# Input stage of a two-network kernel: modulation matmuls of five blocks in rows of eight, and part of the mLSTM keys multiplied in the first two blocks

## The chip, the cores and the metric

The kernel runs on one core of a Trainium2 chip. The metric is the device time of one execution in microseconds (us), as the median of several runs.

## The reference, cut to what matters

Two networks' blocks run one after the other on 256 tokens of width D = 2048. The part that the change touches is the input of the first one: a modulation vector for the tokens and one for the context, a normalised and modulated hidden state for each, and one projection `w_in` whose columns are cut into the inputs of two recurrent mixers (GLA and mLSTM).

```python
mod = (c_act @ w_mod + b_mod)[:, None, :]
mod_c = (cc_act @ w_mod + b_mod)[None, None, :]
sh1, sc1, gt1, sh2, sc2, gt2 = jnp.split(mod, 6, axis=-1)
csh1, csc1, ... = jnp.split(mod_c, 6, axis=-1)
h  = rmsnorm(x, g_norm1) * (1 + sc1) + sh1
hc = rmsnorm(ctx, g_norm1) * (1 + csc1) + csh1
z = jnp.einsum('btd,dp->btp', h, w_in)        # for h and for hc
gq, gk, gv, gg, glr, mq, mk, mv, mo, mgate = jnp.split(z, PROJ_SPLITS, axis=-1)
```

`gk` (GLA keys, 512 columns), `gv` (GLA values, 1024), the gates, and `mk` (mLSTM keys, columns 3600 to 4111 of `w_in`) are needed for tokens and context.

## The kernel before, in words

All inputs are float32. A weight is loaded as 512 KB of raw float32 (`load_raw`, L172; four buffers), cut by ScalarE into a high part `wh` (L187) and by VectorE into the rest `wl` (L188), and a product is made of three matmuls (`mm3`, L208 to L210). VectorE is DVE in the profile, ScalarE ACT, TensorE PE, SyncE SP.

The input stage walks over the 2048 rows of the weights in eight blocks of two k-tiles of 128 rows. For each block, `mod_pe` (L465) computes the modulation of the block's 256 columns for shift and scale, for both vectors at once: four tiles `wm` of 1 MB each hold four k-tiles of `w_mod`; for each of them PE runs a row of four 32-column matmuls into four column strips (L481). After the fourth come a copy by ACT (L486), four transposes (L488), a sum over the strips by DVE (L490) and the bias and gain (L497, L499). `hidden` transposes the tokens (L305) and modulates them (L312, L314), then splits them (L290, L291). `pieces` multiplies the block's weights: GLA keys into four PSUM accumulators that stay open over all blocks; GLA values, two halves, evacuated per block by a copy (block one, L612) or an add (L614) into tiles in SBUF; then the gates (L630). The modulation of block b + 1 is a generator that is stepped between the pieces of block b, at every second piece.

`weights(b, i)` loads the units of a block. Every call of `units` also ticks two background streams: `mods`, which computes the other modulation sections with DVE (L514, L516) from 512 KB loads of `w_mod` and ends each with a bias row on PE (L523), and `side`, recurrent work that fills gaps. What `mods` has not done by the end of the mixing stage is done at once (L1197, `while self.mods_done < 12: self.mods.step()`).

After the eight blocks, `k_evac` (L674) takes GLA's keys out of PSUM by ACT (L678), transposes two of the four (L684), and then the keys stage multiplies the mLSTM keys: `a_form` over all 16 k-tiles, eight units, again with `k_evac`; the queries follow.

The big tiles share one set of 14 buffers of 8 KB per partition (`b8`): the token tiles, the hidden states, the GLA values, the modulation tiles `wm`, later tiles of the recurrences. A tile's first load or write waits for the last reader of the tile that had the buffer before. SP issues the loads in the order in which the program is written; the order of the other engines comes from a scheduler that runs when the program is built. Each engine, SP too, works strictly in its order, so a load that waits for a buffer holds every load behind it.

Of the kernel before, what the change touches and what calls it, by code (L numbers as in the profile page):

```python
# [106 lines left out]
class Kern:  # L107
# [357 lines left out]
    def mod_pe(self, c0, n, secs):  # L465
# [4 lines left out]
        pt = self.psm()[:, :m]  # L470
        for k0 in range(0, 16, 4):
            wm = self.b8((P, 4, m))
            for i, sec in enumerate(secs):
                src = a["w_mod"][0, k0 * P:(k0 + 4) * P, sec * D + c0:sec * D + c0 + n]
                nc.sync.dma_start(wm[:, :, i * n:(i + 1) * n], src.rearrange("(k p) n -> p k n", p=P))

            ins = None
            for j in range(4):
                k = k0 + j
                with self.tc.issue_after(ins) if ins is not None else contextlib.nullcontext():  # L480
                    ins = nc.tensor.matmul(pt[32 * j:32 * j + 32, :], self.cs[:, 2 * k:2 * k + 32], wm[:, j, :],  # L481
                                           start=k < 4, stop=k >= 12, tile_position=(0, 32 * j)).ins
            if k0 < 12:
                yield 1
# [76 lines left out]
    def mix_in(self):  # L561
# [27 lines left out]
        gk_acc = [self.acc() for _ in range(4)]  # L589
        gvc = self.b8((P, 2, 1024))  # L590
# [5 lines left out]
        def mod_block(b):  # L596
            lo, hi = blocks[b]
            return self.mod_pe(lo * P, (hi - lo) * P, (0, 1))
# [7 lines left out]
        def pieces(b):  # L606
# [12 lines left out]
            for half in range(2):  # L619
                for tt in order:  # L620
                    acc = self.ps()
                    self.a_form([acc], [forms[tt]], ws[b, 1 + half], kts[0], kts[-1])
                    add((gvc if tt < 2 else self.gv)[:, tt % 2, half * 512:(half + 1) * 512], acc)
                    yield 1

# [10 lines left out]
        def weights(b, i):  # L636
            if b < nb:
                ws[b, i] = list(self.units(w, 512 + 512 * i, 512, range(*blocks[b])))
# [9 lines left out]
        weights(0, 2)  # L648
        for b in range(nb):
# [7 lines left out]
            for i, _ in enumerate(pieces(b)):  # L657
                if i == 4:
                    weights(b + 1, 1)
                if i == 8:  # L660
                    weights(b + 1, 2)
                if i % 2 == 0:
# [11 lines left out]
        def k_evac(accs, dst, scale):  # L674
            kc = []
            for tt in range(4):
                t = self.t2()
                nc.scalar.activation(out=t, in_=accs[tt], func=AF.Copy, scale=scale)  # L678
# [19 lines left out]
        self.a_form(accs, forms, self.units(w, 3600, 512, range(16)), 0, 15)  # L698
        self.mkc = k_evac(accs, self.mk, float(P) ** -0.5)
# [1155 lines left out]
```

## Time and profile before

| | |
|---|---|
| median of 3 runs | 2664.92 us (2662.52 to 2669.27) |
| profiled execution | 2672.57 us, span 2670.4 us |
| mean granted clock of PE | 0.991 |
| PE busy | 2603.5 us, 97% |
| DVE busy | 1846.4 us, 69% |
| ACT busy | 1281.8 us, 48% |
| queue of SP, share of 16 DMA engines | 63.9%, 548.54 MB |

Busy shares are averages over stages that differ. The input stage is the first 215 us or so of the span. A timeline row gives the start, the length and in brackets the idle time of the engine just before, with what ended it; matmuls overlap their neighbours, so the distance of two starts tells more than a length. "PEclk" is the granted clock as a share of 2.4 GHz; 0.50 is the lower level, 1.2 GHz.

### The profile page before, as it was taken

Reading aid. Unit: us, or ns where it says so; the run is one execution under the profiler, and the core shown is the slowest. Engines: PE = TensorE matmul, PEld = TensorE weight load, DVE = VectorE, ACT = ScalarE, POOL = GpSimd, SP = SyncE. Lnnn points to the kernel's source line nnn. Section 1 sums busy time; section 2 is a strip of 40 time slices with the busy share of each in tenths; the row PEclk is TensorE's granted clock in tenths of the full one; section 3 lists DMA queues with packets and bytes.
Section 4 is the critical chain, followed back from the end, with each engine's and each line's share of the span. In section 5 each row is a group of like instructions: output and inputs, shape, how many; then the busy total and the mean of one; then the engine's idle time right before and its main releaser. Section 6 shows DMA issues by size and latency. Waiting matters only on the chain.

```text
span 2670.4 us, 37499 instructions
## 1 busy us (share of the span) xinstructions
PE 2603.5 (97%) x14093; PEld 2190.4 (82%) x14093; DVE 1846.4 (69%) x3006; ACT 1281.8 (48%) x2008; POOL 26.5 (1%) x52
## 2 busy tenths in 40 slices
PE   5999999999899999999999999999999999999999
PEld 3666888877778888888888988888888889998888
DVE  4466678787778988857856867677755566666665
ACT  2223323344365555544534554555544455657553
POOL 1000000000000000000000000000000000000000
PEclk8999999999999999999999999999999999999999
DMA  9775466678876666666675666556665567645664
GB/s 333 246 239 173 143 211 199 226 224 265 274 260 220 210 220 206 226 218 205 204 243 179 215 190 189 190 189 189 197 232 189 185 208 215 166 143 173 201 217 159
DMA packets 345271, 558.89 MB, mean 209 GB/s; under 512 B 30692, under 2 KB 129178, under 8 KB 342402
## 3 DMA queue, kind: packets, MB, share of 16 engines
q1 hardware_dynamic: 339800, 548.54, 63.9%
q10 hardware_dynamic: 4746, 7.11, 0.7%
q8 instruction: 110, 1.80, 0.3%
q0 software_dynamic: 544, 0.86, 0.1%
q14 instruction: 71, 0.58, 0.1%
HBM read 541.75 MB, written 14.69 MB: 208 GB/s over the span
## 4 chain that ended last, share of the span: by engine, by line
PE 82%; DMA 8%; DVE 6%; ACT 2%; issue 2%; SPq 1%; POOL 0%; ACTq 0%; DVEq 0%
PE acc L237 20%; PE acc L210 10%; PE acc L208 10%; PE acc L209 10%; PE acc L238 10%; PE mod L237 5%; DMA raw<-in_w_in_dram 3%; PE mod L238 2%; PE mod L209 2%; PE mod L210 2%; PE mod L208 2%; DMA raw<-in_w_mod_dram 2%; DVE wl L188 2%; DMA raw<-in_w_out_dram 1%; DVE ev L516 1%
## 5 line engine op out<-in xcount | busy, mean ns | idle before, releaser
L188 DVE TENSOR_TENSOR wl<-raw,wh 128x1024 fp32r<-128x1024 f32 (+4 forms) x804 | 965.7, 1205 | 578.2 <-ACT wh L187 575.5
L187 ACT CAST wh<-raw 128x1024 fp32r<-128x1024 f32 (+4 forms) x804 | 829.6, 1036 | 1068.0 <-PE acc L210 345.7
L237 PE MATMUL acc<-b,wh 128*128 128x512 f32 x2336 | 821.1, 394 | 0.0
L238 PE MATMUL acc<-b,wl 128*128 128x256 f32 x2336 | 634.4, 281 | 1.1 <-DVE wl L188 1.0
L208 PE MATMUL acc<-wh,b 128*128 128x512 f32 (+3 forms) x1580 | 585.3, 373 | 10.0 <-ACT b L290 7.6
L209 PE MATMUL acc<-wl,b 128*128 128x512 f32 (+3 forms) x1580 | 586.6, 371 | 7.5 <-DVE wl L188 7.3
L210 PE MATMUL acc<-wh,b 128*128 128x512 f32 (+3 forms) x1580 | 576.2, 370 | 1.1 <-DVE b L291 0.6
L237 PEld LDWEIGHTS acc<-b,wh 128*128 128x128 f32 x2336 | 434.1, 188 | 88.9 <-issue 0.7
L238 PEld LDWEIGHTS acc<-b,wl 128*128 128x128 f32 x2336 | 438.9, 188 | 15.0 <-DVE wl L188 2.4
L208 PEld LDWEIGHTS acc<-wh,b 128*128 128x128 f32 x1580 | 298.8, 189 | 71.8 <-ACT b L290 9.4
L209 PEld LDWEIGHTS acc<-wl,b 128*128 128x128 f32 x1580 | 299.2, 189 | 62.1 <-DVE wl L188 12.6
L210 PEld LDWEIGHTS acc<-wh,b 128*128 128x128 f32 x1580 | 297.0, 189 | 55.6 <-DVE b L319 4.0
L516 DVE SCALAR_TENSOR_TENSOR ev<-raw,cs,ev 128x512 f32<-128x512 f32 x240 | 179.4, 747 | 59.1 <-DMA raw<-in_w_mod_dram 56.4
L237 PE MATMUL mod<-b,wh 128*128 128x512 f32 x576 | 215.5, 396 | 0.6 <-DVE t L249 0.6
L238 PE MATMUL mod<-b,wl 128*128 128x256 f32 x576 | 161.5, 280 | 0.7 <-DVE wl L188 0.7
L237 PEld LDWEIGHTS mod<-b,wh 128*128 128x128 f32 x576 | 108.4, 188 | 23.5 <-DVE t L249 1.1
L1367 DVE SCALAR_TENSOR_TENSOR t<-t,convw,t 128x189 f32<-128x189 f32 (+2 forms) x344 | 126.9, 423 | 0.0
L238 PEld LDWEIGHTS mod<-b,wl 128*128 128x128 f32 x576 | 108.3, 188 | 3.9 <-DVE wl L188 1.1
L208 PE MATMUL mod<-wh,b 128*128 128x512 f32 (+2 forms) x274 | 96.9, 354 | 0.0
L209 PE MATMUL mod<-wl,b 128*128 128x512 f32 (+2 forms) x274 | 96.7, 353 | 0.0
L210 PE MATMUL mod<-wh,b 128*128 128x512 f32 (+2 forms) x274 | 96.5, 352 | 0.0
L290 ACT CAST b<-t 128x256 fp32r<-128x256 f32 x123 | 47.2, 405 | 64.2 <-DVE t L314 44.1
(357 smaller groups left out, 2469.0 us busy)
## 6 DMA issues: line engine op xcount, KB each, us to landing
raw<-in_w_up_dram SPq DMA_DIRECT2D x160, 512.0 KB, 4.5
raw<-in_w_mod_dram SPq DMA_DIRECT2D x128, 512.0 KB, 4.5
raw<-in_pool_w_in_dram SPq DMA_DIRECT2D x128, 512.0 KB, 3.8
raw<-in_w_in_dram SPq DMA_DIRECT2D x96, 512.0 KB, 4.9
raw<-in_w_down_dram SPq DMA_DIRECT2D x83, 512.0 KB, 4.8
b<-in_w_mod_dram SPq DMA_DIRECT2D x64, 512.0 KB, 7.9
raw<-in_pool_w_out_dram SPq DMA_DIRECT2D x64, 512.0 KB, 4.0
raw<-in_ple_w_gate_dram SPq DMA_DIRECT2D x64, 512.0 KB, 3.9
```

What stands on the lines that cost most here:

```text
L187: nc.scalar.copy(wh[:, :n], raw[:, :n])
L188: nc.vector.tensor_tensor(out=wl[:, :n], in0=raw[:, :n], in1=wh[:, :n].bitcast(F32), op=ALU.subtract)
L208: mm(out, lh, rh, start=first, stop=False)
L209: mm(out, lh, rl, start=False, stop=False)
L210: mm(out, ll, rh, start=False, stop=last)
L237: mm(acc, wh[:, i, o], f.both(kt), start=kt == k_first, stop=False)
L238: mm(acc[:, :T], wl[:, i, o], f(kt)[0], start=False, stop=kt == k_last)
L290: nc.scalar.copy(h, src)
L516: nc.vector.scalar_tensor_tensor(out=ev, in0=rv[:, i, :], scalar=cc, in1=ev, op0=ALU.mult, op1=ALU.add)
L1367: nc.vector.scalar_tensor_tensor(out=ov[:, r0:r1, c0:c1], in0=uv[:, r0 + dy:r1 + dy, c0 + dx:c1 + dx], scalar=tap(ky, kx), in1=ov[:, r0:r1 ...
```

## The change

The modulation function gets a flag that is set for blocks three to seven. With it, two `wm` tiles are loaded before one row of eight matmuls, the newer tile's four first. The first two blocks load a fourth unit of weights (columns 3600 to 4111 of `w_in`) and multiply it, 24 matmuls a block; the result goes into a new tile `mk0` in the set of 14 buffers, by copies in block one and adds in block two. The keys stage then starts at k-tile 4 (six units in place of eight), and its evacuation adds `mk0` on DVE before ACT's scaling.

```diff
--- before.py
+++ after.py
@@ -462,24 +462,32 @@
             self.rows_T([cw[r0:r1, :]] + last, self.convw, r0)
         self.convb = self.convw[:, 9 * NFC:]
 
-    def mod_pe(self, c0, n, secs):
+    def mod_pe(self, c0, n, secs, pairs):
 
 
         nc, a = self.nc, self.a
         m = n * len(secs)
         pt = self.psm()[:, :m]
+        wms = []
         for k0 in range(0, 16, 4):
             wm = self.b8((P, 4, m))
             for i, sec in enumerate(secs):
                 src = a["w_mod"][0, k0 * P:(k0 + 4) * P, sec * D + c0:sec * D + c0 + n]
                 nc.sync.dma_start(wm[:, :, i * n:(i + 1) * n], src.rearrange("(k p) n -> p k n", p=P))
+            wms.append(wm)
+            if pairs and len(wms) == 1:
+                yield 1
+                continue
 
             ins = None
-            for j in range(4):
-                k = k0 + j
-                with self.tc.issue_after(ins) if ins is not None else contextlib.nullcontext():
-                    ins = nc.tensor.matmul(pt[32 * j:32 * j + 32, :], self.cs[:, 2 * k:2 * k + 32], wm[:, j, :],
-                                           start=k < 4, stop=k >= 12, tile_position=(0, 32 * j)).ins
+            for wm, k1 in ((wms[-1], k0), (wms[0], k0 - 4))[:len(wms)]:
+                for j in range(4):
+                    k = k1 + j
+                    with self.tc.issue_after(ins) if ins is not None else contextlib.nullcontext():
+                        ins = nc.tensor.matmul(pt[32 * j:32 * j + 32, :], self.cs[:, 2 * k:2 * k + 32], wm[:, j, :],
+                                               start=k0 < 8 and k1 == k0 if pairs else k0 == 0,
+                                               stop=k0 == 12 and (k1 < k0 or not pairs), tile_position=(0, 32 * j)).ins
+            wms = []
             if k0 < 12:
                 yield 1
         ev = self.t2()[:, :m]
@@ -587,6 +595,9 @@
 
         gates = self.t2((112, 2, T))
         gk_acc = [self.acc() for _ in range(4)]
+
+        early = 2
+        mk0 = self.b8((P, 4, 512))
         gvc = self.b8((P, 2, 1024))
         self.gv = self.b8((P, 2, 1024))
 
@@ -595,7 +606,7 @@
 
         def mod_block(b):
             lo, hi = blocks[b]
-            return self.mod_pe(lo * P, (hi - lo) * P, (0, 1))
+            return self.mod_pe(lo * P, (hi - lo) * P, (0, 1), 1 < b < nb - 1)
 
         def hidden(b, ti):
             kts = list(range(*blocks[b]))
@@ -622,6 +633,12 @@
                     self.a_form([acc], [forms[tt]], ws[b, 1 + half], kts[0], kts[-1])
                     add((gvc if tt < 2 else self.gv)[:, tt % 2, half * 512:(half + 1) * 512], acc)
                     yield 1
+            if b < early:
+                for tt in order:
+                    acc = self.ps()
+                    self.a_form([acc], [forms[tt]], ws[b, 3], kts[0], kts[-1])
+                    add(mk0[:, tt, :], acc)
+                    yield 1
 
             acc = self.ps().rearrange("p (i t) -> p i t", i=2)[:112]
             for i, hx in enumerate((hc, hl)):
@@ -635,7 +652,7 @@
         ws = {}
         def weights(b, i):
             if b < nb:
-                ws[b, i] = list(self.units(w, 512 + 512 * i, 512, range(*blocks[b])))
+                ws[b, i] = list(self.units(w, 512 + 512 * i if i < 3 else 3600, 512, range(*blocks[b])))
         for _ in mod_block(0):
             pass
         hidden(0, 0)
@@ -646,6 +663,7 @@
         weights(0, 1)
         wg = self.gate_weights(w)
         weights(0, 2)
+        weights(0, 3)
         for b in range(nb):
             mods = mod_block(b + 1) if b + 1 < nb else iter(())
 
@@ -659,6 +677,8 @@
                     weights(b + 1, 1)
                 if i == 8:
                     weights(b + 1, 2)
+                    if b + 1 < early:
+                        weights(b + 1, 3)
                 if i % 2 == 0:
                     next(mods, None)
                 if i == 8 and b + 1 < nb:
@@ -671,11 +691,15 @@
         self.gkq = self.b8((P, 2, 4, T))
         self.queries = False
 
-        def k_evac(accs, dst, scale):
+        def k_evac(accs, dst, scale, part=None):
             kc = []
             for tt in range(4):
                 t = self.t2()
-                nc.scalar.activation(out=t, in_=accs[tt], func=AF.Copy, scale=scale)
+                if part is None:
+                    nc.scalar.activation(out=t, in_=accs[tt], func=AF.Copy, scale=scale)
+                else:
+                    nc.vector.tensor_tensor(out=t, in0=accs[tt], in1=part[:, tt, :], op=ALU.add)
+                    nc.scalar.mul(t, t, scale)
                 if tt < 2:
                     kc.append(t)
                     continue
@@ -695,8 +719,8 @@
         self.side.set(self.gla_context(gkc, gvc), SIDE["keys"])
         self.mk = self.t4((P, 4, T))
         accs = [self.acc() for _ in range(4)]
-        self.a_form(accs, forms, self.units(w, 3600, 512, range(16)), 0, 15)
-        self.mkc = k_evac(accs, self.mk, float(P) ** -0.5)
+        self.a_form(accs, forms, self.units(w, 3600, 512, range(2 * early, 16)), 2 * early, 15)
+        self.mkc = k_evac(accs, self.mk, float(P) ** -0.5, mk0)
 
 
         self.side.set(self.gla_scores(), SIDE["queries"])
```

In the order of PE, at the turn from block one to block two, before. L481 are the modulation rows, L630 the gates, L488 the transposes of the modulation, `acc` the GLA keys (of block two here), `ps` other products:

```order
L210 MATMUL ps_424<-wh_256,b_11_120 128x512
L481 MATMUL mod_272<-b_71_342,cs 32x512 x4
L630 MATMUL ps_432<-b_11_120,t_53_246 112x256 x4
L630 MATMUL ps_432<-b_15_124,t_53_246 112x256 x4
L488 MATMUL mod_272<-cst,t_72_349 128x128 x4
L481 MATMUL mod_454<-b_93_455,cs 32x512 x4
L208 MATMUL acc_131<-wh_262,b_15_124 128x512
L209 MATMUL acc_131<-wl_263,b_15_124 128x512
L208 MATMUL acc_132<-wh_262,b_15_124 128x512
L209 MATMUL acc_132<-wl_263,b_15_124 128x512
L208 MATMUL ps_487<-wh_315,b_15_124 128x512
```

And with the change, where L487 is the row, L496 the transposes, the products `ps_445`, `ps_453` and `ps_461` are of the mLSTM keys:

```order
L210 MATMUL ps_437<-wh_257,b_11_120 128x512
L487 MATMUL mod_279<-b_75_349,cs 32x512 x4
L208 MATMUL ps_445<-wh_263,b_15_124 128x512
L209 MATMUL ps_445<-wl_264,b_15_124 128x512
L210 MATMUL ps_445<-wh_263,b_15_124 128x512
L208 MATMUL ps_445<-wh_263,b_15_124 128x512
L209 MATMUL ps_445<-wl_264,b_15_124 128x512
L210 MATMUL ps_445<-wh_263,b_15_124 128x512
L496 MATMUL mod_279<-cst,t_76_356 128x128 x4
L208 MATMUL ps_453<-wh_263,b_15_124 128x512
L209 MATMUL ps_453<-wl_264,b_15_124 128x512
L210 MATMUL ps_453<-wh_263,b_15_124 128x512
```

Six rows further on, where the first GLA keys of block two come:

```order
L208 MATMUL ps_461<-wh_263,b_11_120 128x512
L209 MATMUL ps_461<-wl_264,b_11_120 128x512
L210 MATMUL ps_461<-wh_263,b_11_120 128x512
L208 MATMUL acc_131<-wh_269,b_15_124 128x512
L209 MATMUL acc_131<-wl_270,b_15_124 128x512
```

Six products of block one's mLSTM keys now stand between the last row and the transposes. Behind the transposes come 18 more, the first 12 of them ahead of the first GLA keys of block two (`acc`), and the gates only after them.

In the order of PE, the first two modulation rows of block eight, before, and the bias row of the mods stream:

```order
L210 MATMUL ps_1463<-wh_1283,b_18_127 128x512
L481 MATMUL mod_1430<-b_267_1431,cs 32x512 x4
L481 MATMUL mod_1430<-b_268_1450,cs 32x512 x4
L523 MATMUL ps_1475<-ev_1025,cst 1x512
L208 MATMUL ps_1495<-wh_1283,b_18_127 128x512
```

And with the change:

```order
L210 MATMUL ps_1540<-wh_1360,b_18_127 128x512
L487 MATMUL mod_1507<-b_282_1508,cs 32x512 x4
L487 MATMUL mod_1507<-b_283_1527,cs 32x512 x4
L531 MATMUL ps_1552<-ev_1102,cst 1x512
L208 MATMUL ps_1572<-wh_1360,b_18_127 128x512
```

The rows still stand together, and the bias row behind them.

In the order of SP, the loads of block eight's modulation tiles (b8, two loads each) and those around them, before, with the numbers of tiles:

```order
L475 DMA b8_267_1431<-in_w_mod_dram 128x4x256 x2
L475 DMA b8_268_1450<-in_w_mod_dram 128x4x256 x2
L172 DMA raw_270_1471<-in_w_mod_dram 128x2x512
L525 DMA t2_272_1477<-in_b_mod_dram 1x512
L172 DMA raw_274_1482<-in_w_in_dram 128x2x512
L475 DMA b8_277_1488<-in_w_mod_dram 128x4x256 x2
L475 DMA b8_280_1511<-in_w_mod_dram 128x4x256 x2
L172 DMA raw_286_1546<-in_w_mod_dram 128x2x512
L172 DMA raw_287_1550<-in_w_in_dram 128x2x512
```

And with the change:

```order
L476 DMA b8_282_1508<-in_w_mod_dram 128x4x256 x2
L476 DMA b8_283_1527<-in_w_mod_dram 128x4x256 x2
L172 DMA raw_285_1548<-in_w_mod_dram 128x2x512
L533 DMA t2_287_1554<-in_b_mod_dram 1x512
L172 DMA raw_289_1559<-in_w_in_dram 128x2x512
L476 DMA b8_292_1565<-in_w_mod_dram 128x4x256 x2
L476 DMA b8_295_1588<-in_w_mod_dram 128x4x256 x2
L172 DMA raw_301_1623<-in_w_mod_dram 128x2x512
L172 DMA raw_302_1627<-in_w_in_dram 128x2x512
```

The order is the same, but the buffers are not. Before, the first and third of the four tiles have one buffer and the second and fourth another, so that the third waits for the first's row. With the change all four have the same one, and each waits for the row of the tile before it.

## Rows read from the trace of the kernel before

**Rows 1.** The page's first part: busy time and share of each engine.
```profile
PE 2603.5 (97%) x14093; PEld 2190.4 (82%) x14093; DVE 1846.4 (69%) x3006; ACT 1281.8 (48%) x2008; POOL 26.5 (1%) x52
```

**Rows 2.** Windows: time, PE, PEld, DVE, ACT, POOL busy, then PEclk, DMA share, GB/s.
```profile
64.00:68.00 4.00, 1.65 (x4) 1.36 (x5) 3.27 (x8) 2.11 (x6) 0.00 (x0) 0.71 1.08 392
68.00:72.00 4.00, 4.00 (x10) 3.11 (x10) 0.61 (x2) 0.12 (x1) 0.00 (x0) 0.50 1.05 362
72.00:76.00 4.00, 4.00 (x18) 3.15 (x16) 0.00 (x0) 0.00 (x0) 0.00 (x0) 0.94 0.10 30
```

**Rows 3.** PE's timeline: start, us, engine, line, operation, out<-in, count, [idle before].
```profile
62.85 1.06 PE L481 MATMUL mod<-b,cs 128*32 128x512 f32 x8 [0.44 <-DVE sm L490]
66.35 0.80 PE L208 MATMUL acc<-wh,b 128*128 128x512 f32 x1 [2.44 <-ACT b L290]
66.94 0.63 PE L209 MATMUL acc<-wl,b 128*128 128x512 f32 x1
67.37 0.63 PE L208 MATMUL acc<-wh,b 128*128 128x512 f32 x1
67.80 0.63 PE L209 MATMUL acc<-wl,b 128*128 128x512 f32 x1
...
72.06 0.59 PE L209 MATMUL acc<-wl,b 128*128 128x512 f32 x1
...
74.13 0.39 PE L208 MATMUL acc<-wh,b 128*128 128x512 f32 x1
74.36 0.40 PE L209 MATMUL acc<-wl,b 128*128 128x512 f32 x1
```

**Rows 4.** PE's timeline about a modulation row of four (eight records).
```profile
76.00 0.39 PE L210 MATMUL acc<-wh,b 128*128 128x512 f32 x1
76.31 1.07 PE L481 MATMUL mod<-b,cs 128*32 128x512 f32 x8
77.31 0.50 PE L208 MATMUL acc<-wh,b 128*128 128x512 f32 x1
77.65 0.39 PE L209 MATMUL acc<-wl,b 128*128 128x512 f32 x1
```

**Rows 5.** PE's timeline about a modulation row of eight.
```profile
51.58 1.92 PE L481 MATMUL mod<-b,cs 128*32 128x512 f32 x16
53.44 0.66 PE L305 MATMUL ps<-cst,b 128*128 128x128 f32 x4
```

**Rows 6.** PE's timeline, block eight's modulation to its first matmul.
```profile
194.70 1.92 PE L481 MATMUL mod<-b,cs 128*32 128x512 f32 x16
196.99 1.02 PE L523 MATMUL ps<-ev,cst 128*1 128x512 f32 x2 [0.37 <-DVE ev L516]
...
201.29 1.06 PE L481 MATMUL mod<-b,cs 128*32 128x512 f32 x8 [0.30 <-DMA b<-in_w_mod_dram]
...
205.72 1.06 PE L481 MATMUL mod<-b,cs 128*32 128x512 f32 x8
...
215.16 0.50 PE L208 MATMUL acc<-wh,b 128*128 128x512 f32 x1 [0.34 <-ACT b L290]
```

**Rows 7.** SP's timeline over the same modulation's loads: issues.
```profile
174.40 4.89 SPq L475 DMA_DIRECT2D b<-in_w_mod_dram  x4
...
195.82 2.02 SPq L475 DMA_DIRECT2D b<-in_w_mod_dram  x4
```

**Rows 8.** DVE's timeline at the end of block seven.
```profile
205.62 0.49 DVE L514 TENSOR_SCALAR ev<-raw,cs 128x512 f32<-128x512 f32 x1 [0.93 <-DMA raw<-in_w_mod_dram]
206.02 0.68 DVE L614 TENSOR_TENSOR b<-ps,b 128x512 f32<-128x512 f32 x1
...
214.13 0.54 DVE L314 TENSOR_SCALAR t<-ps,mod,mod 128x256 f32<-128x256 f32 x1
```

**Rows 9.** The chain at the end of the mixing stage: start, length, what.
```profile
730.69 10.66 DMA raw<-in_w_mod_dram
```

**Rows 10.** PE's timeline at the end of the mixing stage.
```profile
725.81 1.84 PE L543 MATMUL ps<-cst,ev 128*128 128x2 f32 x8 [4.41 <-DVE ev L516]
```

## The prediction

> **What bounds the kernel now.** I read the page's first part, then the core's windows through the input stage, then TensorE's (PE's) timeline at each edit, then the queue of SP, then VectorE (DVE). PE is busy 97% of the span [rows 1], so work taken off another engine is worth nothing and an idle microsecond of PE is a lost one, unless a later wait gives it back. The input stage has two parts. Until 72 us the loads are the limit: the DMA engines are full in every window shown up to there, and PE waits and then runs at half clock, 0.50 granted from 68 to 72 us [rows 2]. From 72 us DMA is nearly idle in the window shown and PE sets the time. "Within 0.3%" is 8 us here, about what can be told from no change.
>
> The profiled execution took 2672.57 us, 7.65 more than the median of the runs, 2664.92. The sum below is made against 2672.57 and 7.65 is then taken off.
>
> **The early key products, at the front.** The change moves 48 matmuls of 512 columns from the keys stage into blocks one and two, 24 each. Their number is unchanged, so at full clock they cost PE nothing. They pay where they stand in a hole. The hole is the turn from block one to block two: PE waits 0.44 us for DVE before one modulation row and 2.44 us for ScalarE's (ACT's) cast of the new hidden tokens, then starts matmuls 0.43 us apart instead of 0.23 [rows 3]. Fourteen matmuls start at the slow spacing between 66.35 and 72.06, which costs 14 x 0.20 = 2.8 us. The order rows of PE after the change put 12 of the new matmuls between the transposes of block two's modulation and the first matmul that needs the new hidden tokens, and move a modulation row away from there. Before, the transposes ended and the tokens were ready some 2.9 us of waiting and one row of 1.0 us later, 3.9 us; 12 x 0.23 = 2.8 us covers all but 1.1, and with so short a wait PE should not fall to half clock. Gain: 0.44 + 2.44 - 1.1 + 2.8 = **-4.6 us**. What the step adds: two loads of 512 KB, ahead of others on a full DMA. At the 392 GB/s of [rows 2] each takes 1.3 us, and if all of it shows, 2.7 us of the gain are gone. I count it at nothing, because the longer PE work of these blocks gives the later tiles the same time; without that cover the term is -2. The eight copies and adds of 0.68 us on DVE [rows 8] lie beside PE work. Range -6 (the wait covered whole) to -1 (late, and half the slow stretch back).
>
> **The rows of eight.** A row of four stands between two triples: from the last matmul before it to the second one after it are 77.65 - 76.00 = 1.65 us, of which two normal spacings are 0.46, so a row costs 1.19 us [rows 4]. A row of eight, found in the old program where two rows happened to meet, takes 1.86 us to the next matmul, against 1.00 for the row of four [rows 4, 5]; so eight cost 1.19 + 0.86 = 2.05, and each pair saves 2 x 1.19 - 2.05 = 0.33 us. There are ten pairs (two in each of five blocks) and one is cut apart by gate matmuls in the new order: **-3.1 us**, range -4 to 0. A pair needs two tiles at once, so a tile's load may be later than before; between the first pair's row and the second are some 30 matmuls, 7 us, against 5.4 us for a load (next part). That covers it.
>
> **The last block's modulation.** This is the cost that the diff does not show. The new tile mk0 lives in the same set of 14 buffers as the modulation tiles, from block one until the keys are done. The order rows of SP and the order of buffers say what this does for block eight, which is not paired: its four tiles A, B, C, D had two buffers, and now have one. B's load can only be issued after A's row has read the buffer, while PE's order has B's row right behind A's. Before, A and B had landed long ago, and SP issued C and D together when the rows of A and B were through [rows 6, 7].
>
> I reckon from T0, the end of A's row. How long a load of 1 MB takes when its issue is awaited: C was issued at 195.82 and its row began at 201.29 after a wait for it [rows 6, 7], 5.4 us with D queued behind. The other bound is 1.05 MB at 392 GB/s [rows 2], 2.7 us, with no latency at all; I take 5.4, since it is the same transfer.
> By the Trainium skill (DMA: Bandwidth & Descriptors, Anatomy of one DMA) a transfer, on the path through GpSimd, takes a fixed 2.0 us plus its bytes at 436 GB/s. That makes an estimate of 4.4 us for such a tile, and the sum below would be 1 us lower; the trace's 5.4 us has other loads beside it.
> - B lands at T0 + 5.4. PE idles that long and then runs at half clock. Row B ends at T0 + 6.5, and only then is C issued, to land at T0 + 11.9. PE meanwhile has one bias row of 1.0 us and 12 matmuls at 0.43, 5.1 us: row C at about T0 + 12.6, over at T0 + 13.6.
> - D is issued then and lands at T0 + 19.0; 24 matmuls cover that.
> - Behind D on SP stand the weights of block eight and the mods stream's loads. Before, from D's issue (the third of four issues that start at 195.82, about 196.8) to the first matmul of block eight at 215.16 were 18.3 us, through D's row, a raw load that DVE waited for until 205.62, and DVE's normalising at 214.13 [rows 6 to 8]. The same from T0 + 13.6 gives T0 + 31.9.
> Before, T0 was about 195.7 and block eight's first matmul 19.5 us later. So +12.4. After the second idle PE is at half clock again for about as long as at the front, of which I charge 1.1 of 2.8 us, because PE has another wait there anyhow. **+13.5 us.** Bounds: only B's wait less the old waits that go away, +3; C idle as well and the whole half clock, +19. Counting from D's row instead of its issue gives +10.
>
> **Keys to queries.** The keys' evacuation gains four adds of DVE, 0.68 us each [rows 8], ahead of ACT's scaling. Gla's state matmuls wait for the last of them, since the state tile takes mk0's buffer. The queries' matmuls cover most; I take **+1.5**, from 0 to +5.
>
> **The mods stream.** Its loads step with the weight units, and the keys stage has two units fewer. The two steps are made up in the burst that ends the mixing stage, where PE waits 4.41 us for DVE at 725.81 and one load stands 10.66 us on the chain [rows 9, 10]. Two loads at 1.3 us on the path: **+2.5**, from 0 (the burst hidden) to +6 (half such a turn more).
>
> **Sum:** -4.6 - 3.1 + 13.5 + 1.5 + 2.5 = +9.8; 2672.57 + 9.8 - 7.65 = 2674.7, say **2675 us**.
>
> **The rivals.**
> 1. *Not slower: the last block absorbs its single buffer.* If DVE's chain does not wait behind D, the stall is B's wait of 5.4 less the waits of 0.37 and 0.30 that it replaces and others like them, +3, and the two tails are hidden: -4.6 - 3.1 + 3 = -4.7, **2660 us**. It decides for "not slower" as soon as the last block loses under 8 us with the tails at nothing. For: VectorE has idle time in that stretch. Against: [rows 8] show that it did wait for the raw load behind D. With the front at -6, the pairs at -4 and the last block at +2 it goes to 2657, the edge of faster by over 0.3%.
> 2. *In between.* The stall counted from D's row, +10, and one tail hidden: -4.6 - 3.1 + 10 and 1.5 or 2.5, +4 to +5, **2669 to 2670 us**.
> 3. *The tails bite.* The forecast's stall, with the keys turn at +5 and the burst at +6: **2682 us**; with the last block at +19 up to 2687.
> 4. *The pairs stall.* If second pairs' tiles land later than the 30 matmuls, each of ten pairs costs its load less 7 us and a fall to half clock instead of saving 0.33; two such stalls of 3 us add 6: **2681 us**.
>
> **Chances.** Forecast 0.34 (2671 to 2679), rival 1 0.26, rival 2 0.18, rivals 3 and 4 together 0.22. Slower by over 0.3% begins at 2673: nearly all of rivals 3 and 4 and 0.8 of the forecast, 0.48. Faster by over 0.3% ends at 2657, the better half of rival 1 with several terms at their good ends: 0.14. Within: 0.38. The range from 2657 to 2687 leaves out the best of rival 1 and the worst of 3 and 4. The likeliest case alone has 2671 to 2679.
>
> **What would show it.** In the new profile: a wait of about 1 us in place of 2.44, and no window at 0.50 clock, at the first block's turn; rows of eight in blocks three to seven with nothing idle before them; in the last block B's row 5 us or more behind A's, released by a load, a half clock window behind it, and about 32 us from A's row to block eight's first matmul. If A's and B's rows still stand together, or the distance stays near 20 us, the main term is wrong and rival 1 holds. If a row of eight waits for a load, it is rival 4.

## The result, and the profile after

| | before | with the change |
|---|---|---|
| median | 2665.64 us (2662.52 to 2669.27, 4 runs) | 2705.99 us (2704.56 to 2708.22, 4 runs) |
| ratio | | 1.0152, 95% interval 1.0134 to 1.0169 |
| profiled execution | 2672.57 us, span 2670.4 | 2706.64 us, span 2704.6 |

The change costs 40 us where 10 were forecast, and lies outside the range. The stall in the last block came as forecast. What was missed lies 400 us later, in a stage whose code the change does not touch.

The page's first part of the changed kernel, against [rows 1]: PE's share has not moved, which is why such a share cannot be read as "nothing waits".

```profile
PE 2615.3 (97%) x14093; PEld 2198.5 (81%) x14093; DVE 1855.4 (69%) x3018; ACT 1282.1 (47%) x2007; POOL 26.2 (1%) x52
```

Where the 34 us of the two profiled executions lie can be told by four landmarks that stand in both programs: the first row of block eight's modulation (called A), the last row of the mLSTM's sums (L1120, L1144 in the new numbering; the end of the recurrences), the first row scale of the second network (L1335, now L1359), and the end. The early matmuls moved 48 x 0.23 = 11.0 us across A, and are taken off or added on. Each kernel has one trace, and executions of the kernel before alone lie between 2662.5 and 2677.8 us, so a difference of a few us in one stretch tells little.

| stretch | before | after | difference, moved work taken off |
|---|---|---|---|
| start to A | 194.7 | 205.3 | -0.5 |
| A to the last L1120 | 379.0 | 380.8 | +12.9 |
| last L1120 to first L1335 (mixing stage, feed-forward) | 930.2 | 944.8 | +14.6 |
| first L1335 to the end of the span | 1166.6 | 1173.7 | +7.1 |

The last line is the second network, which nothing here reaches; it comes up again at the end.

**The turn from block one to block two.** The windows that answer to [rows 2], in the changed kernel:

```profile
64.00:68.00 4.00, 2.87 (x13) 1.96 (x12) 3.85 (x10) 0.66 (x2) 0.00 (x0) 1.00 1.08 379
68.00:72.00 4.00, 4.00 (x19) 3.24 (x18) 2.59 (x6) 2.62 (x6) 0.00 (x0) 1.00 1.09 377
72.00:76.00 4.00, 4.00 (x28) 2.92 (x30) 1.92 (x2) 0.00 (x0) 0.00 (x0) 1.00 0.54 156
```

PE's timeline there, which answers to [rows 3]:

```profile
64.46 0.50 PE L208 MATMUL ps<-wh,b 128*128 128x512 f32 x1 [0.35 <-DVE b L623]
...
66.91 0.50 PE L208 MATMUL ps<-wh,b 128*128 128x512 f32 x1 [0.78 <-DVE b L623]
...
68.41 0.39 PE L208 MATMUL acc<-wh,b 128*128 128x512 f32 x1
```

The wait of 2.44 us is gone, two of 0.35 and 0.78 us (1.13 together; 1.1 was forecast) stand in its place, and the window at 0.50 is at full clock.

Most of the gain is gone again at A. In block five PE waits twice for DVE at the transposes of a later stage's weights (L382) and runs at 0.50 of the clock behind that, from 158 to 161 us; the kernel before has no such wait there:

```profile
156.53 0.26 PE L382 MATMUL ps<-cst,t 46*128 46x46 f32 x1 [0.53 <-DVE convw L383]
...
157.86 0.80 PE L208 MATMUL ps<-wh,b 128*128 128x512 f32 x1 [1.08 <-DVE convw L383]
```

**The last block.** PE's timeline with the four rows and block eight's first matmul, against [rows 6]:

```profile
205.27 1.07 PE L487 MATMUL mod<-b,cs 128*32 128x512 f32 x8
211.98 1.93 PE L487 MATMUL mod<-b,cs 128*32 128x512 f32 x8 [5.65 <-DMA b<-in_w_mod_dram]
215.39 1.86 PE L531 MATMUL ps<-ev,cst 128*1 128x512 f32 x2 [1.48 <-DVE ev L524]
...
221.11 1.07 PE L487 MATMUL mod<-b,cs 128*32 128x512 f32 x8
...
228.32 1.07 PE L487 MATMUL mod<-b,cs 128*32 128x512 f32 x8
...
239.34 0.80 PE L208 MATMUL acc<-wh,b 128*128 128x512 f32 x1 [4.47 <-ACT b L290]
```

And SP's timeline, against [rows 7]:

```profile
188.94 0.92 SPq L476 DMA_DIRECT2D b<-in_w_mod_dram  x2
...
206.39 0.92 SPq L476 DMA_DIRECT2D b<-in_w_mod_dram  x2
207.41 0.45 SPq L172 DMA_DIRECT2D raw<-in_w_mod_dram  x1
...
213.97 9.19 SPq L476 DMA_DIRECT2D b<-in_w_mod_dram  x4
223.26 0.45 SPq L172 DMA_DIRECT2D raw<-in_w_mod_dram  x1
```

B's row starts 6.7 us after A's, behind a load; its 1.93 us for eight records, where A's took 1.07, show the half clock. SP issues A's two loads at 188.94 and B's only at 206.39, when A's row is through; C's and D's take it 9.19 us from 213.97, for the same reason. The raw loads stand behind, at 207.41 and 223.26. From A's row to block eight are 34.1 us against 20.5.

**The end of the mixing stage.** PE's timeline, against [rows 10]:

```profile
640.40 0.80 PE L208 MATMUL acc<-wh,b 128*128 128x512 f32 x1 [5.05 <-ACT b L322]
...
732.52 0.95 PE L551 MATMUL ps<-cst,ev 128*128 128x2 f32 x8
...
752.51 1.84 PE L551 MATMUL ps<-cst,ev 128*128 128x2 f32 x8 [10.63 <-DVE ev L524]
```

In the kernel before, the bias row of the last section but one of the mods stream stands here:

```profile
700.37 0.95 PE L543 MATMUL ps<-cst,ev 128*128 128x2 f32 x8
```

There the last section begins at 700 and is waited for at 725.81 for 4.41 us. With the change it begins at 732.52, 20.0 us before its own bias row rather than 25.4, and PE waits 10.63. DVE, on which that row waits, spread the section's sixteen operations (two for each of its eight loads) over 703 to 725 us before; here they stand nearly back to back from 738.27 to 752.36:

```profile
738.27 0.48 DVE L522 TENSOR_SCALAR ev<-raw,cs 128x512 f32<-128x512 f32 x1
...
738.78 6.28 DVE L524 SCALAR_TENSOR_TENSOR ev<-raw,cs,ev 128x512 f32<-128x512 f32 x8
...
750.83 1.53 DVE L524 SCALAR_TENSOR_TENSOR ev<-raw,cs,ev 128x512 f32<-128x512 f32 x2
```

And a wait of 5.05 us for ACT at the start of the stage (640.40) has no counterpart before. From the last L1120 to the first L1335 PE is idle for 29.5 us in place of 20.2 (the length of the stretch less PE's busy time, 915.3 and 910.0).

A third wait stands ahead of that stage, between A and the last L1120: 4.32 us for a step of `side` on DVE, where the kernel before, shown second, has 1.38:

```profile
402.80 3.08 PE L1029 MATMUL ps<-b 128*128 128x128 f32 x16 [4.32 <-DVE b L1022]
```
```profile
414.58 1.13 PE L1005 MATMUL ps<-b 128*128 128x128 f32 x8 [1.38 <-DVE b L998]
```

### The profile page after: what moved, and what is told of

The parts are those of the page before. It is cut to its first block, busy times and chain, and to the rows that moved or that the text cites. A ratio compares the mean times of both kernels' runs of the same rounds, so it can differ in the third digit from the quotient of the medians.

```text
span 2704.6 us, 37508 instructions
## 1 busy us (share of the span) xinstructions
PE 2615.3 (97%) x14093; PEld 2198.5 (81%) x14093; DVE 1855.4 (69%) x3018; ACT 1282.1 (47%) x2007; POOL 26.2 (1%) x52
## 4 chain that ended last, share of the span: by engine, by line
PE 85%; DMA 7%; DVE 4%; ACT 2%; issue 1%; SPq 1%; POOL 0%; ACTq 0%; DVEq 0%
PE acc L237 19%; PE acc L210 11%; PE acc L208 11%; PE acc L209 11%; PE acc L238 10%; PE mod L237 5%; PE mod L238 2%; DMA raw<-in_w_mod_dram 2%; PE mod L209 2%; PE mod L208 2%; PE mod L210 2%; DMA raw<-in_w_in_dram 2%; DVE wl L188 1%; PE ps L208 1%; DVE ev L524 1%
## 5 line engine op out<-in xcount | busy, mean ns | idle before, releaser
L208 PE MATMUL acc<-wh,b 128*128 128x512 f32 (+3 forms) x1564 | 578.6, 373 | 16.9 <-ACT b L290 9.3
L210 PE MATMUL acc<-wh,b 128*128 128x512 f32 (+3 forms) x1564 | 570.6, 371 | 0.7 <-DVE b L291 0.4
```

The costliest lines, as they stand in the source:

```text
L208: mm(out, lh, rh, start=first, stop=False)
L210: mm(out, ll, rh, start=False, stop=last)
```

## The experiments

Four stood against each other at first: the single buffer of the last block, the two steps that the mods stream loses (its lag), the rows of eight, and the early matmuls themselves. "Distance" below is from A's row to block eight's first matmul (20.5 us before, 34.1 with the change), "A to L1120" is the difference of that stretch to the kernel before, moved work added on, and "stretch" the length from the last L1120 to the first L1335 (930.2 and 944.8). "Position" is how many loads the mods stream has issued, in the order of SP, when the first weights of the mixing stage are loaded, and in brackets how many of those are of the section it is in. A section is eight loads; the expectation of e12 calls sixteen a section.

| kernel | median, us | ratio to before, 95% interval | distance | A to L1120 | stretch | position |
|---|---|---|---|---|---|---|
| before | | 1 | 20.5 | | 930.2 | 75 (3) |
| the change | 2705.99 | 1.0152 (1.0134 to 1.0169) | 34.1 | +12.9 | 944.8 | 73 (1) |
| e1 parked | 2695.64 | 1.0084 (1.0071 to 1.0098) | 17.1 | +7.8 | 945.4 | 73 (1) |
| e2 steps back | 2681.96 | 1.0039 (1.0025 to 1.0053) | 33.3 | +5.9 | 927.8 | 75 (3) |
| e3 pairs alone | 2673.90 | 1.0008 (0.9997 to 1.0019) | 20.7 | +1.1 | 928.7 | 75 (3) |
| e4 early alone | 2708.49 | 1.0137 (1.0122 to 1.0153) | 32.1 | +16.0 | 947.4 | 73 (1) |
| e5 parked, steps back | 2671.20 | 1.0004 (0.9991 to 1.0016) | 20.6 | -4.1 | 926.5 | 75 (3) |
| e6 two steps fewer | 2685.48 | 1.0062 (1.0042 to 1.0083) | 17.8 | -2.0 | 943.0 | 73 (1) |
| e7 buffer held | 2688.41 | 1.0073 (1.0052 to 1.0094) | 32.1 | +12.2 | 926.2 | 75 (3) |
| e8 two steps more | 2676.61 | 1.0022 (1.0010 to 1.0035) | 20.9 | -5.8 | 941.2 | 77 (5) |
| e9 held and fewer | 2708.66 | 1.0144 (1.0125 to 1.0163) | 32.1 | +12.9 | 944.8 | 73 (1) |
| e10 e5 without pairs | 2674.86 | 1.0014 (1.0003 to 1.0024) | 20.4 | 0.0 | 926.9 | 75 (3) |
| e11 parked, faster rate | 2697.40 | 1.0109 (1.0090 to 1.0128) | 18.3 | +7.0 | 946.2 | 73 (1) |
| e12 a section ahead | 2693.05 | 1.0088 (1.0075 to 1.0101) | 21.0 | +25.7 | 923.0 | 91 (3) |

The kernel before ran at 2668 to 2671 us beside e1 to e12, so medians are compared by the ratio. Costs in us below are the ratio less 1, or the difference of two ratios, times 2670; by the intervals they are sure to some 3 to 7 us.

**e1, the early sums parked in DRAM.**

```diff
+        mk0d = self.dram.tile([4, P, 512], F32, name="mk0d")
...
+            if b == early - 1:
+                for tt in range(4):
+                    nc.scalar.dma_start(mk0d[tt], mk0[:, tt, :])
...
+        mk1 = self.b8((P, 4, 512))
+        nc.sync.dma_start(mk1, mk0d.rearrange("t p n -> p t n"))
...
-        self.mkc = k_evac(accs, self.mk, float(P) ** -0.5, mk0)
+        self.mkc = k_evac(accs, self.mk, float(P) ** -0.5, mk1)
```

> The changed kernel, but the early sums mk0 go to DRAM after block two and come back into a buffer of the same set at the start of the keys stage, so that block eight's modulation tiles have two buffers again, as before the change. Theory (single buffer): the 5.65 us that PE waited for tile B and most of the 4.47 us before block eight go away, and the distance from A's row to the first matmul of block eight, 34.1 us in the changed kernel, falls back to 20 to 22 us; the time falls by 12 to 15 us to 2691 to 2695 (one load of 1 MB and four small stores are added, under 3 us if they show). Rival (the stall has another cause, the queue of SP or DVE): the distance stays over 30 us and the time at 2703 to 2709.

The distance fell to 17.1 us and the time by 0.68% of the kernel before, 18 us, a little more than expected. The single buffer is the cause of the stall. The stretch did not move, and A to L1120 fell by only 5.1 us: what comes behind block eight takes longer than with the change, and the wait for `side` is still there (4.53 us, at 396.33).

**e2, the mods stream's two steps given back.**

```diff
+        for _ in range(2):
+            self.mods.tick()
         self.mk = self.t4((P, 4, T))
```

> The changed kernel, with two more steps of the mods stream at the start of the keys stage, so that as many are left for the end of the mixing stage as before the change. Theory (the burst): PE's wait of 10.63 us at the end of that stage goes back towards 4.4 us, and with the half clock around it the time falls by 9 to 13 us, to 2693 to 2697; the last block stays as long as it is. Rival (the burst is long because the stage reaches it in another order, not because of two more loads): a fall of 0 to 4 us, 2702 to 2706.

It fell by 1.13%, 30 us, twice what was expected of it. The last block stayed as it was, the wait at the end of the mixing stage is short again, and the one at its start and the one for `side` are gone. Of the 24.6 us between the two traces 17.0 are in the stretch and 7.0 from A to L1120:

```profile
212.52 1.94 PE L487 MATMUL mod<-b,cs 128*32 128x512 f32 x8 [5.26 <-DMA b<-in_w_mod_dram]
...
239.49 0.80 PE L208 MATMUL acc<-wh,b 128*128 128x512 f32 x1 [4.30 <-ACT b L290]
...
731.44 1.84 PE L551 MATMUL ps<-cst,ev 128*128 128x2 f32 x8 [5.36 <-DVE ev L524]
```

**e3 and e4, the rows of eight alone and the early matmuls alone.**

```diff
-        early = 2
-        mk0 = self.b8((P, 4, 512))
+        early = 0
```
```diff
-            return self.mod_pe(lo * P, (hi - lo) * P, (0, 1), 1 < b < nb - 1)
+            return self.mod_pe(lo * P, (hi - lo) * P, (0, 1), False)
```

(e3 also leaves out the fourth unit's loads and `mk0` in the evacuation, which the first edit makes useless.)

> The kernel before with the rows of eight alone and nothing early. By the prediction's term, -3 us: 2662. Theory now, after the changed kernel's trace showed blocks four to seven no shorter: some of the tiles come later and PE waits or falls to half clock once, so 0 to +3: 2665 to 2668. If the pairs themselves carry the loss, 2675 or more.

> The change without the rows of eight. Its last block has one buffer too, and the mods stream two steps less. Theory (buffer and burst carry the loss, the pairs nearly nothing): 2704 to 2710. Rival (the rows of eight carry a good part): under 2698.

The rows of eight change nothing that can be measured, and the early matmuls bring nearly the whole loss. In e3 a row of eight costs just what was reckoned: from the last matmul before it to the second after it are 81.83 - 79.32 = 2.51 us, less two spacings of 0.23 is 2.05. But one of the later pairs waits for a tile, which takes back what five pairs save:

```profile
79.32 0.39 PE L210 MATMUL ps<-wh,b 128*128 128x512 f32 x1
79.64 1.92 PE L487 MATMUL mod<-b,cs 128*32 128x512 f32 x16
81.49 0.50 PE L208 MATMUL ps<-wh,b 128*128 128x512 f32 x1
81.83 0.39 PE L209 MATMUL ps<-wl,b 128*128 128x512 f32 x1
...
159.66 1.93 PE L487 MATMUL mod<-b,cs 128*32 128x512 f32 x16 [1.63 <-DMA b<-in_w_mod_dram]
```

By SP's order the two tiles of that pair were issued from 148.11, 11.5 us ahead of its row:

```profile
148.11 2.99 SPq L476 DMA_DIRECT2D b<-in_w_mod_dram  x4
```

**e5, both repairs together,** which is e1 and e2 in one kernel.

> Both repairs on the changed kernel: mk0 parked in DRAM, and two more steps of the mods stream at the start of the keys stage. Theory (the single buffer and the shorter mods stream are separate causes, and what is left of the change is a small gain): the two falls add, 18 + 30 us by the ratios of e1 and e2, so 6 to 10 us below the kernel before. Rival (the two overlap, or a third cost stays): at or up to 10 us above the kernel before.

The rival came true: nothing is left over, 1.0004. The two falls do not add to 48 us; they end at the kernel before. Start to A is 202.5 us here, 3.3 less than before with the moved work taken off, and A to L1120 is 4.1 shorter, so a small gain is in this one trace, yet that execution, 2664.45 us, is the fastest of its twelve, and the medians don't show it.

**e6, the lag alone, e7, the buffer alone, and e9, both,** on the kernel before. e7 holds an otherwise unused tile of the set, written and read once each.

```diff
         self.mods.rate = MODS["keys"]
+        self.mods.due = -2.0
```
```diff
+        mk0 = self.b8((P, 4, 512))
+        nc.vector.memset(mk0[:, 0, 0:4], 0.0)
         gvc = self.b8((P, 2, 1024))
...
+        nc.vector.tensor_copy(self.sm([P, 4]), mk0[:, 0, 0:4])
         self.mkc = k_evac(accs, self.mk, float(P) ** -0.5)
```

> The kernel before, unchanged but for the mods stream, which misses two steps at the start of the keys stage, as in the changed kernel. Theory (the mods stream's lag alone costs what e2 got back): 20 to 30 us more than the kernel before, with PE's wait at the end of the mixing stage at 10 to 11 us in place of 4.4, and the second long wait of 5 us for ACT some 110 us earlier. Rival (the lag costs only in the order that the change makes): 0 to 6 us.

> The kernel before with one more tile of the set of 14 held from block one to the end of the keys stage; nothing is multiplied early and no row of eight. Theory (the missing buffer alone makes the last block's stall): A's row and B's row 6 to 7 us apart, first matmul of block eight 32 to 34 us after A's row in place of 20.5, and 12 to 18 us more in all. Rival (the early matmuls or the rows of eight are needed for the stall): distance 20 to 22 us, 0 to 3 us more.

> The kernel before with both side effects of the change and none of its work: one tile of the set of 14 held to the end of the keys stage, and the mods stream two steps short. Theory (the side effects are the whole loss, the moved matmuls and the rows of eight come out near nothing): 16.5 + 19.5 = 36 by e6 and e7, so 30 to 42 us more than the kernel before, as the change has. Rival (the change's own work loses or wins 10 us or more): under 28, or over 50.

e6 costs 16.5 us, less than the 20 to 30 that were expected and far from the rival's 0 to 6, and has both waits of the changed kernel's mixing stage:

```profile
625.59 0.80 PE L208 MATMUL acc<-wh,b 128*128 128x512 f32 x1 [5.81 <-ACT b L322]
...
735.38 1.84 PE L543 MATMUL ps<-cst,ev 128*128 128x2 f32 x8 [10.06 <-DVE ev L516]
```

e7 costs 19.5 us, a little above its band, and makes the stall without a single early matmul:

```profile
198.60 1.07 PE L481 MATMUL mod<-b,cs 128*32 128x512 f32 x8
205.16 1.94 PE L481 MATMUL mod<-b,cs 128*32 128x512 f32 x8 [5.49 <-DMA b<-in_w_mod_dram]
...
230.68 0.50 PE L208 MATMUL acc<-wh,b 128*128 128x512 f32 x1 [3.26 <-ACT b L290]
```

e9 costs 38.4 us: a kernel that does none of the change's work pays what the change pays (the two intervals overlap), with the same four waits.

```profile
205.32 1.93 PE L481 MATMUL mod<-b,cs 128*32 128x512 f32 x8 [5.45 <-DMA b<-in_w_mod_dram]
...
230.89 0.79 PE L208 MATMUL acc<-wh,b 128*128 128x512 f32 x1 [3.23 <-ACT b L290]
...
645.15 0.80 PE L208 MATMUL acc<-wh,b 128*128 128x512 f32 x1 [5.77 <-ACT b L322]
...
757.05 1.84 PE L543 MATMUL ps<-cst,ev 128*128 128x2 f32 x8 [10.44 <-DVE ev L516]
```

**e8, two steps more,** e2's edit on the kernel before.

> The kernel before with two more steps of the mods stream at the start of the keys stage. If each step costs its load in the burst, 10 to 25 us less. If the burst costs by what it happens to wait for, and six loads are hidden as eight are: 0 to 5 us either way.

It is 5.9 us slower, just above the second band. By SP's order six loads of the mods stream stand behind the last weights of the mixing stage in the kernel before, eight with the change and four here (the expectation counts two more in each). Four in place of six gain nothing; the wait for the section is down to 1.44 us, and another of 5.75 us stands right behind it:

```profile
731.50 1.02 PE L543 MATMUL ps<-cst,ev 128*128 128x2 f32 x8 [1.44 <-DVE ev L516]
...
739.10 0.79 PE L208 MATMUL acc<-wh,t 128*128 128x512 f32 x1 [5.75 <-ACT t L322]
```

**e10, e5 without the rows of eight.**

> The kernel of e5 (parked, two steps of mods back) without the rows of eight, that is the early keys alone with both side effects repaired. If the rows of eight gain their 0.33 us each: 2 to 3 us more than e5. If their waits cost what they save, as e3 has it: within 2 us of e5. If the front's gain of 3 to 5 us shows in the end: 2 to 8 us below the kernel before.

It is 0.10% above e5, 2.7 us, as if the rows of eight gained their 0.33 us each here; the two intervals overlap, so it is not settled. Nor is it below the kernel before (1.0014): the gain at the front does not show in the time.

**e11, the lag made good during the mixing stage,** which is e1 with a faster mods stream there.

```diff
-MODS = {"inputs": 1.0, "keys": 1.0, "values": 1.25, "gates": 0.75, "output": 0.5, "ffn": 0.15}
+MODS = {"inputs": 1.0, "keys": 1.0, "values": 1.25, "gates": 0.75, "output": 0.575, "ffn": 0.15}
```

> The parked kernel of e1, whose mods stream is still two steps short when the keys end, but which catches them up during the mixing stage (rate 0.575 in place of 0.5 steps for each unit), so that eight loads are left for its end as before. Theory (the lag costs at the end of the mixing stage, by where the last section of the stream begins): PE's wait there is 4 to 6 us again and the time is within 5 us of e5, 0 to 5 us above the kernel before. Rival (the two steps lost in the keys stage cost by themselves, in the keys and values stages): as e1, 18 to 26 us above the kernel before.

Here the theory fell. The wait at the end is 6.11 us, as it had said, and as many loads are left as before (six), and yet the time is 29 us above the kernel before and the stretch 946.2, as in e1. So neither the number of loads left nor the length of the last wait is the price. The rival is right in part: A to L1120 is 11.1 us longer than in e5, with the wait for `side` in it; but the larger part lies in the mixing stage.

```profile
394.36 3.79 PE L1035 MATMUL ps<-b 128*128 128x128 f32 x16 [4.52 <-DVE b L1028]
...
632.92 0.79 PE L208 MATMUL acc<-wh,b 128*128 128x512 f32 x1 [5.58 <-ACT b L322]
...
745.43 1.84 PE L551 MATMUL ps<-cst,ev 128*128 128x2 f32 x8 [6.11 <-DVE ev L524]
```

The table then says what goes with the stretch: the load of its section at which the mods stream stands when the stage begins. All kernels so far that begin it with three loads of a section issued lie from 926 to 930 us, all others from 941 to 947.

**e12, a section ahead,** made to test that: three loads of a section issued, but two whole sections, 16 loads, further on.

```diff
-MODS = {"inputs": 1.0, "keys": 1.0, "values": 1.25, "gates": 0.75, "output": 0.5, "ffn": 0.15}
+MODS = {"inputs": 1.0, "keys": 1.0, "values": 2.25, "gates": 0.75, "output": 0.5, "ffn": 0.15}
```

> The kernel before with the mods stream a whole section of 16 loads ahead when the mixing stage begins (rate 2.25 in place of 1.25 while the values are multiplied), so that it begins this stage at the same load of a section, the 12th, as the kernel before, e2, e5 and e7, but none of its sections is left for the burst at the end. Theory (the position in the section when the mixing stage begins decides, the number of loads left does not): from the last row of the recurrence to the last bias row of the stream in the mixing stage about 150 us as in those kernels or less, in place of 162 to 167, and PE does not wait 4.4 us at its end; the time from 12 us below the kernel before to 5 above, by what the faster stream costs in the values stage. Rival (the loads left decide): 25 us or more below the kernel before in the mixing stage alone.

The stretch is 923.0 us, 7 less than before, with none of the last section in the burst; so the place in the section goes with the stretch once more, and the rival's 25 us are not there. The time is 23 us worse all the same, beyond what was expected, for the faster stream costs it all and more where it runs: A to L1120 takes 25.7 us longer, with waits for ACT's casts in the values stage.

```profile
401.68 2.07 PE L208 MATMUL acc<-wh,b 128*128 128x512 f32 x4 [6.01 <-ACT wh L187]
...
435.78 2.07 PE L208 MATMUL acc<-wh,b 128*128 128x512 f32 x4 [3.65 <-ACT wh L187]
...
750.29 0.80 PE L208 MATMUL acc<-wh,t 128*128 128x512 f32 x1 [6.52 <-ACT t L322]
```

## Why the prediction was wrong

By stretches of the trace the forecast and the result are: to A, -7.7 (front and rows of eight) against -0.5; A to L1120, +15.0 (last block and keys) against +12.9; the mixing stage, +2.5 against +14.6; the second network, nothing against +7.1. That is +9.8 against +34.1.

**The early matmuls at the front: right where it was read, small in the sum.** The term was -4.6. The turn's wait fell from 2.88 us to 1.13, and the half clock behind it is gone. In the whole front, e5 shows -3.3 us to A and the change -0.5. In the change one row waits 0.51 us for a tile (122.12), but more goes to the waits of 0.53 and 1.08 us in block five and the half clock behind them. The sum held no loss there.

**The rows of eight: right by the row, wrong by the cover.** 2.05 us a row, as reckoned. The step that failed here is "some 30 matmuls, 7 us, against 5.4 us for a load": in e3 the pair at 159.66 had more time than that and still waited 1.63 us, because its two tiles, by SP's order, were issued from 148.11 and landed 11.5 us later, with the DMA engines full from 152 to 160 us (shares of 1.03 and 1.08). So it was the load that was too short in the sum. Rival 4 had the mechanism; it comes once and not ten times, and the term is 0 in place of -3.1. (That term is also nine or ten times 0.33, 3.0 or 3.3.)

**The last block: right by the mechanism, with luck in the sum.** Reckoned from T0, A's end at 206.3: B's row at T0 + 5.7 (forecast 5.4), C's at 14.8 (12.6), D's at 22.0 (19.0), block eight's first matmul at 33.0 (31.9). The term was +13.5, and A to L1120 has +12.9, but not all of that is the buffer's. e2, with the steps given back, has +5.9, and e5, with the buffer given back as well, -4.1: so 7.0 us go with the lag, 10.0 with the buffer, and the remaining -4.1 stood in no term. That the sum agrees so well is in part luck. e7 shows 19.5 for the held buffer by itself, of which 3.9 in its trace stand ahead of A, where its other blocks have a buffer less as well. By the Trainium skill (DMA: Bandwidth & Descriptors, Anatomy of one DMA) the tile would land after an estimated 4.4 us, by the fit for the path through GpSimd. PE's waits of 5.26 to 5.65 us in the five kernels with the held tile, which begin as the tile's loads are issued, are longer, and the measurement decides. The same page's rule for authors (Rules for kernel authors: issue a load early and wait for it late) is what the single buffer makes impossible, and here e1 gives the price of that: 18 us (9 with the steps given back, e2 against e5).

**Keys to queries:** +1.5, for which no run was made. From 240 to 345 us the changed kernel's timeline of PE shows no wait.

**The mods stream: the step that failed.** The text had "+2.5, from 0 (the burst hidden) to +6". It priced two loads at the end of the mixing stage by their bytes. The lag alone costs 16.5 us (e6), and giving it back brings 30 to the change (e2) and 21 to the parked kernel (e5 against e1). What goes with the cost is not two loads (e11, e12) but where the section boundaries fall: all six kernels that begin the mixing stage with one load of a section issued have a wait of 5.05 to 6.33 us for ACT at its start (640.40 with the change, 625.59 in e6, 645.15 in e9, 632.92 in e11), which no other kernel has, and five of the six wait 10 us in place of 4 to 6 at its end. All six also have the wait for `side` ahead of the stage, at 2.47 to 4.53 us, where the others have 1.38 at most. With the stall of the buffer the lag makes up the loss: e9.

Why one or five loads of a section are worse than three was not shown. The trace has what is waited for, ACT's casts behind raw loads in the four buffers that weights and the mods stream share; that the section's change, with DVE's short work and the next section's loads, collides with the first weights of the stage is argued from the timeline and not tried by itself. Nor do the parts add to better than some 10 us: e1 and e2 give 48 together, e6 and e7 36, the change has 40. Part of that is seen: from A to L1120 the lag costs 7.0 us in the change and 11.9 in the parked kernel (e1 against e5), and nothing in the kernel before (e6, -2.0). The units that were moved take two ticks from `side` as well, and no run gives those back; e5 lacks them and is level with the kernel before, so by themselves they cost nothing that can be told, but what they add to the lag is open.

**The range** was too narrow because this term looked at the burst alone. Its bound was half a turn of 10.66 us [rows 9], and that load starts at 730.69, 4.9 us behind the bias row that ends the burst (725.81), so it is not one of the burst's. What the lag does at the start of the stage and ahead of it was not in the sum at all.

No version beat the kernel before: e5 and e3 cannot be told from it.

## What to carry to other kernels

A tile that is kept over a loop takes a buffer from whatever rotates in the same set: list, for each load of the loop, which reader frees its buffer and what stands behind it in its queue. A background stream that is paced by work units changes its phase everywhere behind the place where units are taken out; price that by the stages that it shares loads and engines with, and give the units' ticks back when work is moved. Test side effects by themselves on the old kernel (e6, e7, e9): that is what told the cost of the side effects from that of the work.

## What was not expected of the hardware

In the second network, from 1600 to 1800 us, PE is busy all the time at full clock in every kernel, with the same instructions, and yet it gets through fewer of them in the changed kernel: 570 and 571 records in 100 us against 575 before.

```profile
1600.00:1700.00 100.00, 100.00 (x575) 87.61 (x574) 68.71 (x98) 50.67 (x76) 0.15 (x1) 1.00 0.60 189
1700.00:1800.00 100.00, 100.00 (x575) 87.66 (x574) 71.94 (x102) 50.92 (x77) 0.30 (x2) 1.00 0.59 189
```

```profile
1600.00:1700.00 100.00, 100.00 (x570) 87.11 (x570) 72.06 (x110) 52.29 (x82) 0.15 (x1) 1.00 0.59 181
1700.00:1800.00 100.00, 100.00 (x571) 87.22 (x570) 72.71 (x104) 49.73 (x76) 0.30 (x2) 1.00 0.62 194
```

That is 0.8%, and it goes with the last line of the first table. The kernels with the tile of the early sums, or one like it, have 570 to 574 there (the change, e1, e2, e4, e5, e7, e9, e10, e11), those without it 575 to 577 (before, e3, e6, e8, e12). Their second networks take 3.1 to 7.1 us and 1.0 to 2.1 us longer than before, in one trace each. Whether the place of the tiles in memory or the execution itself is the cause stays open.
